# A decoder trunk in fp32 on one core: the end of its mixing layer by a table of units, two merge sums on VectorE, and eight columns in an existing slot

## The chip, the cores and the metric

The kernel runs on one core of one Trainium2 chip. The metric is device time in microseconds of one execution. Engines are named as in the profile: PE (TensorE matmul) and PEld (its weight loads), DVE (VectorE), ACT (ScalarE), POOL (GpSimd), SP (SyncE, which here issues most of the loads).

## The reference

One layer of a decoder trunk and a last norm, on x of 1 x 1024 x 1024 in float32:

```
h  = rmsnorm(x) @ w_in             # attention inputs and two gates of 1024 columns
ya = differential attention (4 heads x 2 x 64, causal, ALiBi)
yb = sliding-window attention (8 heads of 64, window 128, sinks)
m  = sigmoid(g0) * (ya @ w_br_da) + sigmoid(g1) * (yb @ w_br_sw)   # merge
x  = x + m @ w_mix_out             # mixing layer
u  = rmsnorm(x) @ w_up             # to 2 x 2816 columns
c  = causal depthwise conv of width 3 over u, plus bias
x  = x + (silu(gate) * val) @ w_down
out = rmsnorm(x)
```

## The kernel before

**Arithmetic.** Every float32 operand of a product is held as two fp32r tiles, high and low: a cast on ACT makes the high part and a subtraction on DVE the low part. A product takes three matmuls (high x high, high x low, low x high). The large products with weights are done by a scheme of seven products P1 to P7 in place of eight, on blocks A11, A12, A21, A22 of the weights and B11, B12, B21, B22 of the data: some factors are sums of blocks (S1 to S4 of the weights, T1 to T4 of the data), and the results are recombined. Data lie transposed: a partition is a channel, a tile of 128 channels by 1024 positions has two halves of 512.

**The merge** (`rest`, L839 to L875) makes m in eight steps of 128 channels. A step loads two gate tiles (`gr`), multiplies them by the norm's scale on POOL (L845), takes the sigmoid on ACT (L852), computes the two branch products on PE (L199 to L201, tiles `sc` and `g` in PSUM), gates them on DVE (L859, L861), and sums the two (L869, into `mr`): on POOL for steps 0 to 6, on DVE for step 7. Then it splits blocks of the sum into high (L882, ACT) and low (L883, DVE), and from step 4 on adds blocks in place by an accumulating DMA on POOL's queue (L889).

**The mixing layer** (`mix`, L891 to L1033) runs the seven products in the order P1, P2, P5, P6, P3, P7, P4, each in two halves: 14 halves, i = 0 to 13. A half loads and splits a weight (L178 cast on ACT, L180 low part on DVE), runs 24 matmuls (L1014) into two PSUM chains and adds them to the residual tile `xm[m]` on DVE (L1016). A chain of PSUM is used again by a later stage and so must be evicted first. A half of `xm[m]` becomes final in P2 (m = 0 to 3, first half), P3 (second half), P7 (m = 4 to 7, second half) and P4 (first half). `finish` then stores it (L935), squares it on ACT (L942) and adds the square to a sum on POOL (L943).

**The data of the up projection** are made from these finished halves, in code that `finish` puts off by one to three halves with `later`. For m < 4 the first half times the norm's weight gives B11 (L945), the second times the negative weight (`nw`, 8 columns; L947) is added to the first by an accumulating DMA (L930), and the sum is split into T1. For m > 3 the second half times the weight goes to a tile c (L951) and gives B22; it is added to both halves of `xm[m - 4]`, which gives T3 and T2. The first half times the negative weight (L956) gives B21, and added again T4. `put` splits a result: a cast on ACT (L919) and a low part on DVE (L920). T3 and B21 are put in tiles that the trace calls x0 to x7. `run_due(i)` runs what is due at half i, ahead of that half's matmuls; what is due at 14, 15 and 16 comes after the last.

**The first weights of the up projection** come from `part_pair` (L116): part 0 is A11 and A12, part 1 S1 and S2, part 2 S3 and S4, part 3 A22; each is a load on SP (L121), a cast on ACT (L126) and a low part on DVE (L128). Parts 1 and 2 are called in the two halves of P4 ahead of `run_due`, with a raised priority, parts 0 and 3 after P4.

**The up projection** (`hidden`, L1047) does for its first block of columns (j = 0) P1, P5, P3, P7, P2, then the sums of squares (L207), P6 and P4; a product is L1043. Then P1 and P2 of j = 1 follow, and the norm's scale is spread over the partitions by eight transposes (L222). The sums are recombined (L512 to L521) and go on to a scaling on POOL and the convolution.

**Order.** A scheduler reorders instructions of one engine by priority and by its own estimate of times; `tc.issue_after(x)` keeps an instruction behind x, `tc.high_priority` raises it. Semaphores for the data are added by the framework. Each engine works its list strictly in order. Pools give out buffers by tag and size, and an instruction that takes a buffer again waits for the last reader.

## Time and profile before

| | us |
|---|---|
| runs | 1348.41, 1350.07, 1350.72; median 1350.07 |
| the profiled execution | 1351.85 |
| its span in the trace | 1350.1, at a mean granted clock of 0.99 |
| the merge's last step and the mix's start | around 590 to 600 |
| the mix's end and the first products of the up projection | around 660 to 720 |

The span runs from the first to the last instruction; the execution's time holds 1.75 us more. Times in the text are microseconds from the span's start. A row of a timeline gives the start, the duration (of the whole group where it ends in x2 or more, first start to last end), engine, line, operation, output and inputs; in square brackets the time for which the engine idled before, and what ended that. A row of the waits gives who waited on whom: total, number, longest.

### The profile page before, as it was taken

What the parts mean: (1) busy time and instruction counts of PE and PEld (TensorE: products, weight loads), DVE (VectorE), ACT (ScalarE), POOL (GpSimd) and SP (SyncE); (2) the same over time, 40 slices, a digit from 0 to 9 for tenths busy, and PEclk for the clock granted to TensorE, in tenths of its full rate; (3) what the DMA queues carried; (4) which work ended last, traced back from release to release, by engine and by line L of the source; (5) the groups of instructions that cost most, each with busy time, mean ns of one, the idle gap of its engine ahead of it and who ended that gap; (6) DMA issues with size and microseconds to landing.
All of it is one profiled execution on the core that took longest, in us unless ns stands there. A gap on an engine that the chain in (4) does not pass through costs nothing.

```text
span 1350.1 us, 17338 instructions
## 1 busy us (share of the span) xinstructions
PE 1324.8 (98%) x6162; PEld 1088.5 (81%) x6162; DVE 1036.6 (77%) x1503; ACT 639.0 (47%) x1010; POOL 512.1 (38%) x412
## 2 busy tenths in 40 slices
PE   9999999999999999999969999999999999999997
PEld 7888888888888878878858888888888888888886
DVE  8836763389888975457579998989999988886855
ACT  9423232276667773335654343334333444554543
POOL 0447664001101016753355567766766622000002
PEclk9999999999999999999979999999999999999999
DMA  8356976966553245578694336554635227953434
GB/s 303 130 154 200 262 190 187 294 177 187 141 138 140 78 132 199 151 222 231 179 252 141 140 121 176 142 189 121 218 100 146 71 87 268 313 174 116 154 93 144
DMA packets 86598, 231.67 MB, mean 172 GB/s; under 512 B 9584, under 2 KB 17392, under 8 KB 86256
## 3 DMA queue, kind: packets, MB, share of 16 engines
q1 hardware_dynamic: 63264, 187.04, 41.4%
q0 software_dynamic: 10368, 26.22, 11.4%
q10 hardware_dynamic: 12880, 17.31, 3.7%
q8 instruction: 48, 0.79, 0.2%
q14 instruction: 38, 0.31, 0.1%
HBM read 173.39 MB, written 84.41 MB: 191 GB/s over the span
## 4 chain that ended last, share of the span: by engine, by line
PE 87%; POOL 4%; DMA 3%; DVE 2%; issue 2%; ACT 1%; SPq 0%; POOLq 0%; ACTq 0%; DVEq 0%
PE t L1043 44%; PE y L1263 9%; PE d L1263 7%; PE m L1014 4%; PE g L199 3%; PE g L200 3%; PE g L201 3%; PE sc L687 3%; POOL mr L869 2%; DMA gr<-gd 2%; POOL gr L845 2%; DMA xm<-xm 1%; PE t L703 1%; PE t L806 1%; PE sc L775 1%
## 5 line engine op out<-in xcount | busy, mean ns | idle before, releaser
L180 DVE TENSOR_TENSOR wl<-raw,wh 128x1024 fp32r<-128x1024 f32 (+2 forms) x91 | 100.0, 1100 | 70.9 <-ACT wh L178 58.2
L178 ACT CAST wh<-raw 128x1024 fp32r<-128x1024 f32 (+2 forms) x91 | 80.5, 884 | 111.8 <-PE y L1263 53.6
L157 ACT CAST sh<-sf 128x1024 fp32r<-128x1024 f32 x58 | 60.6, 1050 | 113.8 <-PE t L1043 99.5
L1193 POOL TENSOR_TENSOR us<-us,rstd 128x1024 f32<-128x1024 f32 x42 | 92.3, 2229 | 57.5 <-DVE us L520 31.8
L1043 PE MATMUL t<-T,sh 128*128 128x512 f32 x352 | 111.2, 397 | 0.0
L216 POOL TENSOR_TENSOR rs<-ms,mhalf 128x8 f32<-128x8 f32 (+2 forms) x9 | 13.7, 1519 | 240.6 <-DVE ms L214 234.5
L143 POOL TENSOR_TENSOR sf<-rv 128x512 f32<-128x512 f32 x29 | 53.3, 1837 | 110.2 <-DMA rv<-in_w_up 45.5
L1043 PE MATMUL t<-x,wh 128*128 128x512 f32 x248 | 84.8, 399 | 3.9 <-ACT x L919 3.9
L159 DVE TENSOR_TENSOR sl<-sf,sh 128x1024 fp32r<-128x1024 f32 x58 | 77.9, 1344 | 9.1 <-ACT sh L157 9.1
L1043 PEld LDWEIGHTS t<-T,sh 128*128 128x128 f32 x352 | 66.6, 190 | 15.4
L199 PE MATMUL g<-xh,wh 128*128 128x512 f32 x176 | 71.4, 405 | 1.5 <-ACT g L616 1.5
L200 PE MATMUL g<-x,wh 128*128 128x512 f32 x176 | 70.7, 402 | 0.0
L201 PE MATMUL g<-xh,wl 128*128 128x512 f32 x176 | 70.7, 401 | 0.0
L1210 DVE SCALAR_TENSOR_TENSOR c<-us,vecs,c 128x1024 f32<-128x1024 f32 x44 | 70.3, 1630 | 0.1
L1043 PE MATMUL t<-T,sl 128*128 128x512 f32 x176 | 69.3, 394 | 0.0
L1043 PE MATMUL t<-x,sh 128*128 128x512 f32 x212 | 68.4, 390 | 0.0
L1209 DVE SCALAR_TENSOR_TENSOR c<-us,vecs,c 128x1024 f32<-128x1024 f32 x44 | 66.0, 1537 | 1.2 <-ACT c L1207 1.2
L145 POOL TENSOR_TENSOR sf<-raw,rv 128x512 f32<-128x512 f32 x29 | 54.2, 1869 | 32.0 <-DVE sl L159 32.0
L1263 PE MATMUL y<-h,wh 128*128 128x512 f32 (+1 forms) x224 | 66.3, 379 | 0.0
L1014 PE MATMUL m<-x,wh 128*128 128x512 f32 x192 | 61.4, 401 | 1.8 <-DVE gr L861 1.8
L691 DVE CUSTOM_DVE_ANT_0 L<-sc,bias 128x128 f32<-128x128 f32 (+7 forms) x64 | 47.7, 752 | 17.0 <-PE sc L687 14.2
L670 POOL MEMSET aT<- 128x128 f32 x32 | 6.2, 205 | 142.9 <-PE t L716 102.0
(338 smaller groups left out, 4016.6 us busy)
## 6 DMA issues: line engine op xcount, KB each, us to landing
u<-qd SPq DMA_DIRECT2D x72, 256.0 KB, 6.1
raw<-in_w_in SPq DMA_DIRECT2D x22, 512.0 KB, 5.5
raw<-in_w_up SPq DMA_DIRECT2D x22, 512.0 KB, 4.7
hd<-c SPq DMA_DIRECT2D x22, 512.0 KB, 2.6
sdP<-in_w_down POOLq DMA_DIRECT2D x16, 704.0 KB, 8.3
rv<-in_w_up SPq DMA_DIRECT2D x20, 512.0 KB, 4.9
hc<-hd SPq DMA_DIRECT2D x33, 256.0 KB, 4.8
gr<-gd SPq DMA_DIRECT2D x16, 512.0 KB, 4.6
```

Of the source, the lines that this page charges most:

```text
L159: low = nc.vector.tensor_tensor(lo, src, hi.bitcast(F32), ALU.subtract)
L178: self.hi = nc.scalar.copy(wh, raw)
L180: self.lo = (eng or nc.vector).tensor_tensor(wl, raw, wh.bitcast(F32), ALU.subtract)
L199: nc.tensor.matmul(ps, wh[:, kc + o, :], ah, start=first and n == 0, stop=False)
L200: nc.tensor.matmul(ps, wh[:, kc + o, :], al, start=False, stop=False)
L201: nc.tensor.matmul(ps, wl[:, kc + o, :], ah, start=False, stop=last and n == len(kcs) - 1)
L1014: nc.tensor.matmul(ps, v[:, m % 2 * 4 + k, :], x, start=start and k == j == 0, stop=k == 3 and j == 2, skip_group_check=True)
L1043: nc.tensor.matmul(ps, (ah, ah, al)[p][:, k, :], (bh, bl, bh)[p], start=first and n == p == 0, stop=last and p == 2 and n == len(ks) - 1, ...
L1193: i = (nc.vector if m % NF == 0 else nc.gpsimd).tensor_tensor(us[:, 2:], us[:, 2:], self.rstd, ALU.mult)
L1209: nc.vector.scalar_tensor_tensor(c, us[:, 1:T + 1], cw[1], c, ALU.mult, ALU.add)
L1210: nc.vector.scalar_tensor_tensor(c, us[:, 0:T], cw[0], c, ALU.mult, ALU.add)
L1263: nc.tensor.matmul(ps, v[:, k - k0, :], x, start=start and k == i == 0, stop=k == HK - 1 and i == 2, skip_group_check=True)
```

## The change

**1. Merge sums.** L869 runs on DVE for steps 6 and 7 instead of step 7 alone.

**2. `nw`** is taken from the tag "ms" of its pool, whose tile of eight columns exists already (in `rstd_cols`), instead of a buffer of its own.

**3. The put-off work** is no longer collected in `finish`. Small functions for one unit each stand in a table `due`, by half: which function, for which k, in which order.

**4. B21** is made straight from the residual tile: the cast multiplies by `nw` (L921), and one DVE instruction multiplies and subtracts (L922). The scaled half for the addition is made apart (`scale3`), in the other half of the same tile.

**5. The first weights.** Part 0 (A11, A12) is called in half 13 ahead of `run_due`, parts 1 and 2 in the halves of P4 behind it, part 3 behind everything.

**6. Evictions** of halves 11 and 12 are kept behind the low part that `run_due` made last (`held`), those of the others behind the weight's low part (`first`), as is `finish` in half 13.

```diff
-                    (nc.vector if m == KC - 1 else nc.gpsimd).tensor_tensor(mr[:, m], gs[0], gs[1], ALU.add)
+                    (nc.vector if m > KC - 3 else nc.gpsimd).tensor_tensor(mr[:, m], gs[0], gs[1], ALU.add)
...
-        nw = self.st.tile([P, KC], F32, name="nw")
+        nw = self.tl(self.st, [P, KC], "ms")
...
-        later = lambda i, f: due.setdefault(i, []).append(f)
...
-            if m < 4 and hf == 0:
-                later(i + 2, lambda: (nc.scalar.mul(x, x, wcol(m)), put("B11", k, x)))
-            elif m < 4:
-                later(i + 2, lambda: (nc.scalar.mul(x, x, nw[:, m:m + 1]), add(col(k, 0), x)))
-                later(i + 3, lambda: put("T1", k, col(k, 0)))
-            elif hf:
-                t = x22[k // 2][:, k % 2]
-                later(i + 1, lambda: (nc.scalar.mul(t, x, wcol(m)), put("B22", k, t), add(col(k, 1), t)))
-                later(i + 2, lambda: (add(col(k, 0), t), put("T3", k, col(k, 1))))
-                later(i + 3, lambda: put("T2", k, col(k, 0)))
-            else:
-                t = col(m, 1)
-                later(i + 1, lambda: (nc.scalar.mul(t, x, nw[:, m:m + 1]), put("B21", k, t), add(col(k, 0), t)))
-                later(i + 2, lambda: put("T4", k, col(k, 0)))
+        def scale1(k):
+            x = col(k, 0)
+            nc.scalar.mul(x, x, wcol(k))
+            put("B11", k, x)
+
+        def scale2(k):
+            x = col(k, 1)
+            nc.scalar.mul(x, x, nw[:, k:k + 1])
+            add(col(k, 0), x)
+
+        c22 = lambda k: x22[k // 2][:, k % 2]
+
+        def scale4(k):
+            nc.scalar.mul(c22(k), col(k + 4, 1), wcol(k + 4))
+            put("B22", k, c22(k))
+
+        def sums4(k):
+            add(col(k, 1), c22(k))
+            add(col(k, 0), c22(k))
+
+        def scale3(k):
+            nc.scalar.mul(col(k + 4, 1), col(k + 4, 0), nw[:, k + 4:k + 5])
+            add(col(k, 0), col(k + 4, 1))
+
+        t1, t2, t3, t4 = (lambda k, n=n, h=h: put(n, k, col(k, h)) for n, h in (("T1", 0), ("T2", 0), ("T3", 1), ("T4", 0)))
+        b21 = lambda k: put("B21", k, col(k + 4, 0), nw[:, k + 4:k + 5])
+        due = {6: ((scale1, 0, 1),), 7: ((scale1, 2, 3),), 10: ((scale2, 0, 1),), 11: ((t1, 0, 1), (scale2, 2, 3), (scale4, 0, 1), (sums4, 0, 1)),
+               12: ((scale4, 2, 3), (t1, 2, 3), (sums4, 2, 3), (t3, 0, 1)), 13: ((t3, 2, 3), (t2, 0, 1), (b21, 0), (scale3, 0), (b21, 1), (scale3, 1)),
+               14: ((b21, 2), (t2, 2), (b21, 3), (t2, 3), (scale3, 2, 3), (t4, 0, 1), (t4, 2, 3))}
...
-                        if stage == "P4":
-                            self.uw = uw
-                            w0.update(self.part_pair(pair, 1 + h))
-                            self.uw = None
+                    if i == 13:
+                        w0.update(self.part_pair(pair, 0))
...
                     run_due(i)
+                    held = lows[-1] if lows else None
+                    first = self.lo
+                    if stage == "P4":
+                        self.uw = uw
+                        w0.update(self.part_pair(pair, 1 + h))
+                        self.uw = None
...
-                        tt(x, x, ps, ALU.subtract if o or stage == "P2" else ALU.add)
-                        if done:
-                            finish(i, m + o, hf)
+                        with tc.issue_after((held if 10 < i < 13 else first).ins):
+                            tt(x, x, ps, ALU.subtract if o or stage == "P2" else ALU.add)
+                        if last:
+                            with tc.issue_after(first.ins) if i == 13 else nullcontext():
+                                finish(m + o, hf)
...
-        with tc.high_priority(60):
-            for part in (0, 3):
-                w0.update(self.part_pair(pair, part))
         run_due(i)
-        run_due(i + 1)
-        run_due(i + 2)
+        w0.update(self.part_pair(pair, 3))
```

Lines behind L930 have other numbers after the change: L1014 is L1034, the eviction L1016 is L1037, L919 and L920 are L918 and L919, L942 and L943 are L941 and L942, L947, L951 and L956 are L951, L957 and L965, L1043 is L1061.

How it stands in the engines' lists, first on DVE at the merge's last two steps (a piece of the difference; gr tiles are the gates, x and m the split blocks, wl a weight's low part):

```order
 L859 SCALAR_TENSOR_TENSOR gr_5593<-gr_5593,g_5624 128x512
 L861 TENSOR_TENSOR gr_5593<-gr_5593,g_5638 128x512
+L869 TENSOR_TENSOR mr<-gr_5589,gr_5593 128x1024
 L180 TENSOR_TENSOR wl_5663<-raw_5659,wh_5661 128x1024
 L883 TENSOR_TENSOR x_1013_5653<-mr,x_1013_5653 128x512
 L883 TENSOR_TENSOR m_5136<-mr,m_5136 128x512
```

The sum of step 6 now stands on DVE behind its own last gate and ahead of a weight's low part; on POOL, where it stood behind the two L845 of step 7, it is gone.

Second, DVE where P7's last eviction meets P4's second weight (xm_5769 and xm_5770 are xm6 and xm7, T_0 and T_1 are T1 for k = 0 and 1, B_0 and B_1 are B22), before:

```order
L180 TENSOR_TENSOR wl_6270<-raw_6266,wh_6268 128x1024
L920 TENSOR_TENSOR T_0_5752<-xm_5763,T_0_5752 128x512
L1016 TENSOR_TENSOR xm_5769<-xm_5769,m_5788 128x512
L920 TENSOR_TENSOR T_1_5753<-xm_5764,T_1_5753 128x512
L1016 TENSOR_TENSOR xm_5770<-xm_5770,m_5789 128x512
L180 TENSOR_TENSOR wl_6330<-raw_6326,wh_6328 128x1024
L920 TENSOR_TENSOR B_0_5756<-c_5775,B_0_5756 128x512
L920 TENSOR_TENSOR B_1_5757<-c_5775,B_1_5757 128x512
```

And after:

```order
L180 TENSOR_TENSOR wl_6270<-raw_6266,wh_6268 128x1024
L919 TENSOR_TENSOR T_0_5752<-xm_5763,T_0_5752 128x512
L919 TENSOR_TENSOR T_1_5753<-xm_5764,T_1_5753 128x512
L180 TENSOR_TENSOR wl_6332<-raw_6328,wh_6330 128x1024
L919 TENSOR_TENSOR B_0_5756<-c_5775,B_0_5756 128x512
L919 TENSOR_TENSOR B_1_5757<-c_5775,B_1_5757 128x512
L1037 TENSOR_TENSOR xm_5769<-xm_5769,m_5788 128x512
L1037 TENSOR_TENSOR xm_5770<-xm_5770,m_5789 128x512
```

The two evictions moved behind the weight's low part and the two B22 splits.

Third, ACT from B22's first casts to the first cast of an S part (L126 sh), before (x_1093 and x_1094 are x0 and x1, from T3; c_5775 and c_5776 hold c0, c1 and c6, c7 in the text's words):

```order
L919 CAST B_1_5757<-c_5775 128x512
L935 DMA x2d<-xm_5769 128x512
L942 ACTIVATE sqs<-xm_5769 128x512
L935 DMA x2d<-xm_5770 128x512
L942 ACTIVATE sqs<-xm_5770 128x512
L935 DMA x2d<-xm_5767 128x512
L126 CAST sh_6334<-raw_6332 128x1024
L126 CAST sh_6392<-raw_6390 128x1024
L919 CAST T_2_5754<-xm_5765 128x512
L919 CAST T_3_5755<-xm_5766 128x512
L919 CAST x_1093_6343<-xm_5763 128x512
L919 CAST x_1094_6347<-xm_5764 128x512
```

And after:

```order
L918 CAST B_1_5757<-c_5775 128x512
L918 CAST T_2_5754<-xm_5765 128x512
L918 CAST T_3_5755<-xm_5766 128x512
L918 CAST x_1091_6348<-xm_5763 128x512
L918 CAST x_1092_6351<-xm_5764 128x512
L934 DMA x2d<-xm_5769 128x512
L941 ACTIVATE sqs<-xm_5769 128x512
L934 DMA x2d<-xm_5770 128x512
L941 ACTIVATE sqs<-xm_5770 128x512
L957 ACTIVATE c_5776<-xm_5769,vecs 128x512
L957 ACTIVATE c_5776<-xm_5770,vecs 128x512
L918 CAST B_2_5758<-c_5776 128x512
```

Both S casts left this place: S1 and S2's stands two rows further on, then a store and a square of each of xm4 and xm5, then A11 and A12's (wh), and S3 and S4's behind the T2 and B21 units of half 13. On POOL the four DMAs of c0 and c1 now follow the two of T1 directly, and the four of c6 and c7 each other.

The change to `nw` moves one DVE instruction of 128 x 8 from the program's start to the attention's end, and the scheduler puts the last sliding-window steps (the stretch from 410 to 490 us) in another order on DVE, PE and ACT: the same instructions, differently interleaved.

More of the change, by code (lines that the diff above doesn't have):

```diff
@@ L907, in mix @@
         x22 = [self.tl(self.cpl, [P, 2, H2], "c") for _ in range(2)]
-        nw = self.st.tile([P, KC], F32, name="nw")
+        nw = self.tl(self.st, [P, KC], "ms")
         nc.vector.tensor_scalar(nw, self.vecs[:, C_NF:C_NF + KC], -1.0, None, ALU.mult)
-        acc, nsq = self.rstd, []
+        acc, nsq, lows = self.rstd, [], []
         col = lambda m, hf: xm[m][:, hf * H2:(hf + 1) * H2]
         wcol = lambda m: self.vecs[:, C_NF + m:C_NF + m + 1]
-        due = {}
         def parts(t, src, scale=None):
@@ L919, in parts @@
                 nc.scalar.copy(hi, src)
-                tt(lo, src, hi.bitcast(F32), ALU.subtract)
+                low = tt(lo, src, hi.bitcast(F32), ALU.subtract)
             else:
                 nc.scalar.mul(hi, src, scale)
-                stt(lo, src, scale, hi.bitcast(F32), ALU.mult, ALU.subtract)
+                low = stt(lo, src, scale, hi.bitcast(F32), ALU.mult, ALU.subtract)
+            lows.append(low)
             return hi, lo
@@ L930, in mix, with finish @@
         add = lambda x, y: nc.gpsimd.dma_start(x, y, accum_op=ALU.add)
-        later = lambda i, f: due.setdefault(i, []).append(f)
-        def finish(i, m, hf):
+        def finish(m, hf):
             x, k = col(m, hf), m % 4
@@ L964, in run_due @@
             with tc.issue_after(self.hi.ins), tc.issue_after(self.lo.ins):
-                for f in due.pop(i, ()):
-                    f()
+                for f, *ks in due.pop(i, ()):
+                    for k in ks:
+                        f(k)
         plan = {"P1": ("B11", 1, True, 0, 0, False), "P2": ("B21", 0, True, 0, 0, True), "P5": ("T1", 0, True, 4, 1, False), "P6": ("T2", 1, False, 0, 1, False),
@@ L973, in mix @@
             for n, stage in enumerate(STAGES):
-                b, which, start, o, hf, done = plan[stage]
+                b, which, start, o, hf, last = plan[stage]
                 if stage == "P7":
```

## The prediction

> **What bounds the kernel now.** I read the page first, then PE's waits, then busy time by stage, then the timelines around the waits. The page's busy times, slices and waits of PE:
>
> ```profile
> PE 1324.8 (98%) x6162; PEld 1088.5 (81%) x6162; DVE 1036.6 (77%) x1503; ACT 639.0 (47%) x1010; POOL 512.1 (38%) x412
> PE   9999999999999999999969999999999999999997
> ...
> PE t L1043 <- ACT wh L126: 6.7, 1, 6.7
> PE t L1043 <- ACT x L919: 3.9, 1, 3.9
> PE m L1014 <- DVE gr L861: 1.8, 1, 1.8
> ```
>
> TensorE is busy 98% of the span, and one slice of 40 falls to 6. The three longest waits, 12.4 us together, are all in code that the diff touches: the last merge step (L861), and the mixing layer's end with the first products of the up projection (L126, L919). Busy time and granted clock of the stretches that hold them (length, then PE, PEld, DVE, ACT, POOL, the clock, DMA share and GB/s):
>
> ```profile
> 590.00:600.00 10.00, 8.20 (x34) 6.39 (x34) 6.41 (x9) 3.83 (x6) 5.14 (x3) 0.96 0.65 211
> 600.00:610.00 10.00, 10.00 (x39) 8.01 (x38) 5.67 (x8) 3.43 (x5) 0.88 (x1) 0.86 1.05 356
> ...
> 670.00:680.00 10.00, 5.80 (x25) 4.35 (x24) 9.12 (x9) 6.22 (x11) 5.76 (x6) 0.89 1.07 264
> 680.00:690.00 10.00, 7.53 (x22) 5.99 (x23) 10.00 (x13) 9.01 (x17) 7.21 (x8) 0.60 1.08 252
> 690.00:700.00 10.00, 7.79 (x34) 6.00 (x32) 6.17 (x6) 2.53 (x6) 3.56 (x3) 1.00 1.06 332
> 700.00:710.00 10.00, 8.32 (x30) 7.34 (x31) 5.58 (x7) 6.79 (x10) 5.72 (x4) 0.66 0.57 149
> ```
>
> A full-clock stretch grants 1.00, a half-clock one 0.5: so 0.96 and 0.86 make (0.04 + 0.14) × 10 × 2 = 3.6 us at half clock after the 1.8 us wait; 0.89 and 0.60 make 10.2 us, the last 8 of them up to about 688; 0.66 makes 6.8 us. PE's timeline at the ends of the stages:
>
> ```profile
> 593.92 0.62 PE L1014 MATMUL m<-x,wh 128*128 128x512 f32 x2
> ...
> 598.68 0.73 PE L1014 MATMUL m<-x,wh 128*128 128x512 f32 x2 [1.80 <-DVE gr L861]
> ...
> 675.41 0.40 PE L1014 MATMUL m<-x,wl 128*128 128x512 f32 x1
> 682.47 1.22 PE L1043 MATMUL t<-B,wh 128*128 128x512 f32 x2 [6.66 <-ACT wh L126]
> ...
> 701.68 0.80 PE L1043 MATMUL t<-x,wh 128*128 128x512 f32 x1 [3.89 <-ACT x L919]
> ...
> 718.58 0.63 PE L1043 MATMUL t<-x,wh 128*128 128x512 f32 x2
> ...
> 719.27 1.03 PE L222 MATMUL t<-ident,rs 128*128 128x128 f32 x8
> ```
>
> The last rows give a warm matmul's price: two at 718.58 and one behind them fill the time to 719.27, 0.23 us each. The mix's 336 (14 halves of 24) from 593.92 would end at 671.8; they end at 675.6: 3.9 lost, 1.8 by the wait and half of 3.6 by the clock. From 675.6 to L222 at 719.27 lie 43.6 us: 108 matmuls L1043 (25.0) and some 2 us of L207, so 16.6 are lost: 6.66 + 3.89 waiting, and about (688 − 682.5)/2 + 6.8/2 = 6.2 by the clock. **At most about 21 us are to be had.** After 719.27 I read PE as full, so what is won there stays won.
>
> **The merge end.** The step for m = 6 and the last gate, on POOL, ACT and DVE:
>
> ```profile
> 586.16 4.76 POOL L845 TENSOR_TENSOR gr<-gr,rstd 128x1024 f32<-128x1024 f32 x2 [2.95 <-DMA gr<-gd]
> 590.89 3.37 POOL L869 TENSOR_TENSOR mr<-gr,gr 128x1024 f32<-128x1024 f32 x1
> ...
> 590.95 1.06 ACT L852 ACTIVATE gr<-gr 128x1024 f32<-128x1024 f32 x1 [0.37 <-POOL gr L845]
> ...
> 585.62 0.68 DVE L861 TENSOR_TENSOR gr<-gr,g 128x512 f32<-128x512 f32 x1
> ...
> 594.94 0.69 DVE L883 TENSOR_TENSOR x<-mr,x 128x512 fp32r<-128x512 f32 x1 [2.94 <-ACT x L882]
> ...
> 597.95 0.68 DVE L861 TENSOR_TENSOR gr<-gr,g 128x512 f32<-128x512 f32 x1
> 598.66 1.23 DVE L869 TENSOR_TENSOR mr<-gr,gr 128x1024 f32<-128x1024 f32 x1
> ```
>
> Now the sum's operands are ready at 586.3 (585.62 + 0.68), but it stands on POOL behind two L845 until 590.89 and takes 3.37; its casts follow at 594.3, and DVE's last gate (597.95 to 598.6), which frees the PSUM tile for which PE waits, stands behind the splits L883. On DVE it costs 1.23 and could end at 587.5. The casts then follow the sigmoid of 590.95 on ACT: casts 592.0 to 593.1, splits 592.6 to 593.9, four gates of 0.6, the last done at 596.35. PE wants it at 596.7: no wait. The price that no row shows is this DVE sum beside POOL's L845. Below: 1.23 and POOL unhurt. Above: it blocks and is blocked, as in this pair with its undisturbed like:
>
> ```profile
> 675.45 4.13 DVE L920 TENSOR_TENSOR T<-xm,T 128x512 fp32r<-128x512 f32 x2
> ...
> 681.30 1.28 DVE L920 TENSOR_TENSOR B<-c,B 128x512 fp32r<-128x512 f32 x2
> ...
> 675.76 3.27 POOL L943 TENSOR_TENSOR rstd<-rstd,sqs 128x512 f32<-128x512 f32 x2
> ```
>
> Two DVE splits took 4.13 beside POOL's adds, 1.28 without. So above, the sum ends at 589.8, POOL's second L845 and the sigmoid come a microsecond later, and the last gate ends at 597.35: a wait of 0.65, so short that I expect no half-clock stretch. I win 3.9 less 0.65: **3.2**, between 3.2 and 3.9. The Trainium skill, "SBUF — State Buffer", section "SBUF: two separate sides", states that a DVE operation with two SBUF inputs and a GpSimd operation that reads SBUF share an exclusive port lock for the whole instruction. The 4.13 agrees; by that rule the upper price holds. The skill's "TensorE: Matmul & The Clock Gate", Part 1, would have half clock only after an idle window of about 3.4 us; here 1.80 sufficed, so the row decides.
>
> **The mix's stages.** Their weights, products and evictions keep their places, so they move up with the 3.2, except P7's eviction of xm6 and xm7:
>
> ```profile
> 665.87 0.68 DVE L1016 TENSOR_TENSOR xm<-xm,m 128x512 f32<-128x512 f32 x1
> ...
> 668.67 1.23 DVE L180 TENSOR_TENSOR wl<-raw,wh 128x1024 fp32r<-128x1024 f32 x1 [2.12 <-ACT wh L178]
> ```
>
> It stood ahead of the last weight split (L180); now it stands behind that split and two B22 splits, which wait for ACT's scales, which wait for the second accumulating DMA. By the durations above it ends at about 668.5, where PE (3.2 earlier) wants its PSUM tile at 666.8: **a new wait of 1.75**, with a half-clock stretch some 3.5 in all. I count it at nothing: the up projection cannot start before about 681 anyway, as follows, so the mix may end at 672.4 or 675.9. If that cover were gone it would cost the 3.5.
>
> **The chain to the up projection.** ACT, then POOL's accumulating DMAs and their time from issue to landing (min, median, max):
>
> ```profile
> 664.61 0.62 ACT L919 CAST T<-xm 128x512 fp32r<-128x512 f32 x1 [1.70 <-DMA xm<-xm]
> 665.13 1.33 ACT L947 ACTIVATE xm<-xm,nw 128x512 f32<-128x512 f32 x2
> 666.37 1.32 ACT L951 ACTIVATE c<-xm,vecs 128x512 f32<-128x512 f32 x2
> ...
> 672.09 2.00 ACT L126 CAST sh<-raw 128x1024 fp32r<-128x1024 f32 x2 [1.37 <-DVE xm L1016]
> ...
> 678.07 0.62 ACT L919 CAST x<-xm 128x512 fp32r<-128x512 f32 x1 [2.41 <-DMA xm<-c]
> ...
> 681.39 1.55 ACT L126 CAST wh<-raw 128x1024 fp32r<-128x1024 f32 x2
> ...
> 666.26 1.78 POOL L930 DMA_DIRECT2D xm<-xm  x2 [1.93 <-DVE T L920]
> ...
> DMA to landing us min/median/max: 3.4/6.8/9.7
> ```
>
> Before, ACT cast the S parts (672.09), then waited for x1's sum (T3) to land (678.07), did c6, c7 and B22, and only then cast A11 at 681.39, on which PE's 6.66 ends. After, c0 and c1 lead to six accumulating DMAs in a row on POOL (two T1, four T3 and T2). The second T1 lands at 664.61 − 3.2 = 661.4; one cast, two scales and two c (0.6 + 1.3 + 1.3) later the issues begin at about 663.1, 0.67 apart: x1's T3 is the fifth, issued at 665.7. Its landing I take as 8.1 us, between the median 6.8 and the maximum 9.7 since six are under way: 673.8. Behind it ACT has x1's cast, two squares, c6, c7, two B22, the S1/S2 cast (half of 2.00) and two squares: 10 × 0.6 + 1.0, so A11 is cast from 680.6 to 681.6, against 681.39 to 682.42. The early load of A11 thus gains ACT only 0.8.
>
> The larger change is behind it. PE starts P1 at 681.7. The S3/S4 cast, before done at 674.1, now stands behind six T3, T2 and B21 casts and four scales, and ends near 690.4, its low part 691.9. So P1 and P5 (12 matmuls each, at half clock to 688, then full) end at 690.5 and P3 waits 1.4, ending 694.3; P7 697.0, P2 699.8. **The 3.89 us wait and its 3.4 us of half clock go**, as x6 and x7 are made by one ACT and one DVE instruction straight from xm (L921, L922), ahead of scale3. Then L207 to 701.5, P6 704.3, P4 707.1. Late next is j = 1's first weight (A11, cast behind both S pairs): ready at about 709.8, a wait of 2.7; its products end at 712.6 and, with P2 of j = 1, L222 starts between 714.9 and 716.6, I take 715.2. Against 719.27 that is **−4.1**. The merge's 3.2 is in this sum already (as the start 661.4), not to be added.
>
> **The rest.** The tile nw in a slot of "ms" moves one small DVE instruction (128x8, too short to matter) from the program's start to the attention's end, and with it the scheduler's order of the last sliding-window steps. PE and DVE there:
>
> ```profile
> 410.00:490.00 80.00, 77.91 (x445) 64.75 (x445) 74.41 (x244) 58.78 (x162) 7.36 (x27) 1.00 0.33 106
> ```
>
> PE idles 2.1 of 80 us, so at most 2.1 can be won; DVE is at 93%, so a worse order could lose about as much. I take 0, ±2. B21 by one scaled split instead of scale and split saves nothing that is waited for elsewhere.
>
> **The sum.** 1351.85 (the profiled execution: the span 1350.1 and 1.75 around it) − 4.1 = 1347.75. The profiled execution lies 1.8 over the median of the runs, 1350.07, so against that I predict **1346.0**. A change within 0.2%, 2.7 us, is about what a measurement of this kernel cannot tell from none.
>
> **Rivals.** *Slower: the six DMAs in a row block ACT.* Five transfers precede x1's cast, which stands ahead of all weight casts of the up projection on ACT. Software transfers by queue, 655 to 705:
>
> ```profile
> q0 software_dynamic: 2258, 4.14, 48.3%
> ```
>
> 4.14 MB took 48.3% of 50 us, so five of 16 transfers take 7.6 us if they have the engines to themselves, and landing follows; at half of the engines 15.2 after 663.1, at 678.3, 4.5 later than I assume, which leaves +0.4. Slower by over 2.7 from a landing at 680.6 on; at a share of 0.4 it is 682.1 and +4.2: **1354.2**. For it: the DMA share of 1.06 to 1.08 in these stretches. Against it: the longest of all landings so far was 9.7. Chance 0.18.
>
> *No change: gains are given back.* The merge is won, but P7's eviction and the late S3/S4 cast make new waits, and L222 comes 1 to 2 us earlier or as before: **1349**. For it: the 16.6 us lost are a chain of casts and DMAs on ACT and POOL that the merge doesn't shorten, and DVE is full (10.00 of 10) from 680 to 690. Against it: the wait for x6 and x7 is cut by construction. Chance 0.22.
>
> *A bigger gain.* x1 lands in 5 us instead of 8.1, P1 starts 3 us sooner and j = 1's weight with it; half clock ends earlier: −8.5, **1341.5**. Chance 0.15; the forecast's own case has 0.45 (1343.5 to 1347.3).
>
> **How the numbers follow.** Faster by over 0.2%: 0.45 + 0.15 = 0.60; within: 0.22; slower: 0.18. The range leaves out half of the slower case and the end of the bigger gain: 1340 to 1353.5, which takes in the attention's ±2 and the landing's 6.8 to 9.7.
>
> **What would show it.** Right: in the profile after, no wait of PE on L861 and full clock from 590 to 610; the mix ending between 672 and 676 with a wait of 1 to 2 us for xm6's eviction; a first product of the up projection at 681 ± 2 with a wait for the A11 cast of 6 to 9 us; no wait on x6 or x7; a short wait in P3 and one of 2 to 3 us at j = 1's first weight. Wrong: landings of L930 over 12 us; or a first product before 677, which would mean that the early A11 load decides after all; or a PE idle time over 4 us between 410 and 490.

## The result, and the profile after

The changed kernel takes **1337.77 us** in the median of four runs (1336.39 to 1340.05), the kernel before beside it 1349.58 (1348.41 to 1350.72): a ratio of 0.9914, interval 0.9897 to 0.9931, so 11.8 us faster. That is nearly three times the forecast of 4.1 and 2.2 us below the end of its range. The profiled execution took 1337.29 us, with a span of 1335.5.

The page and PE's longest waits after:

```profile
PE 1307.9 (98%) x6162; PEld 1086.4 (81%) x6162; DVE 1059.9 (79%) x1504; ACT 637.6 (48%) x1010; POOL 513.5 (38%) x411
PE   9999999999999999999979999999999999999997
...
PE t L1061 <- ACT wh L126: 7.0, 2, 5.5
PE m L1034 <- DVE xm L1037: 2.4, 1, 2.4
PE g L199 <- DVE u L518: 1.8, 1, 1.8
PE t L361 <- DVE x L359: 1.5, 1, 1.5
PE t L1061 <- ACT sh L126: 1.4, 1, 1.4
PE g L199 <- ACT g L616: 1.4, 4, 0.5
PE t L1061 <- DVE wl L128: 1.4, 1, 1.4
```

The waits on L861 and on x are gone, and new ones stand in their place: the eviction L1037, the S parts, a weight's low part. PE's *busy* time is 16.9 us less (1324.8 to 1307.9) for the same 6162 records of matmuls. Another order of the units can remove idle time, and stretches at half clock here and there, but those are no fewer at the mix's end: 17.0 us of them from 660 to 720 before, 17.1 after. The stretches after, with the columns of before:

```profile
590.00:600.00 10.00, 10.00 (x46) 8.28 (x45) 8.10 (x11) 3.25 (x4) 0.88 (x1) 1.00 0.94 327
600.00:610.00 10.00, 10.00 (x46) 8.29 (x45) 6.29 (x10) 3.49 (x6) 2.67 (x3) 1.00 1.04 350
660.00:670.00 10.00, 7.64 (x27) 5.87 (x26) 5.43 (x8) 5.24 (x9) 5.27 (x6) 0.83 0.90 177
670.00:680.00 10.00, 4.43 (x16) 2.84 (x16) 6.17 (x8) 7.48 (x12) 5.86 (x7) 0.82 0.76 187
680.00:690.00 10.00, 7.73 (x26) 5.65 (x27) 8.08 (x10) 7.08 (x12) 5.65 (x6) 0.84 0.99 247
690.00:700.00 10.00, 10.00 (x44) 8.22 (x42) 7.14 (x8) 5.13 (x9) 3.99 (x4) 0.83 0.98 263
700.00:710.00 10.00, 7.47 (x35) 5.38 (x34) 4.16 (x6) 3.72 (x5) 0.99 (x3) 1.00 0.54 172
710.00:720.00 10.00, 9.69 (x39) 7.89 (x40) 7.99 (x11) 4.08 (x6) 8.04 (x7) 0.83 0.40 138
```

The merge's end is full and at full clock now. The mix's end still holds 13 us of idle PE (660 to 720), and its half-clock stretches have only moved. PE's timeline after, around it:

```profile
665.65 0.78 PE L1034 MATMUL m<-x,wh 128*128 128x512 f32 x2 [2.36 <-DVE xm L1037]
...
678.49 1.22 PE L1061 MATMUL t<-B,wh 128*128 128x512 f32 x2 [5.53 <-ACT wh L126]
688.04 0.73 PE L1061 MATMUL t<-B,sh 128*128 128x512 f32 x2 [1.43 <-ACT sh L126]
...
717.07 1.03 PE L222 MATMUL t<-ident,rs 128*128 128x128 f32 x8
```

L222 starts at 717.07 against 719.27: of the 14.6 us by which the spans differ, 2.2 have been won here. The rest arises behind it, in the up and the down projection, where PE's list is the same before and after. A piece of the mix in the timelines of before and after:

```profile
629.63 0.62 PE L1014 MATMUL m<-x,wh 128*128 128x512 f32 x2
...
631.72 0.39 PE L1014 MATMUL m<-x,wh 128*128 128x512 f32 x1
```

```profile
629.81 0.62 PE L1034 MATMUL m<-x,wh 128*128 128x512 f32 x2
...
631.17 0.62 PE L1034 MATMUL m<-x,wh 128*128 128x512 f32 x2
```

Before, nine matmuls take 2.09 us (629.63 to 631.72), 0.232 each; after, six take 1.36 (629.81 to 631.17), 0.227 each, both at a granted clock of 1.00. And in before's own merge, six take 1.36 as well:

```profile
590.29 0.39 PE L201 MATMUL g<-yh,wl 128*128 128x512 f32 x1
...
591.65 0.39 PE L201 MATMUL g<-yh,wl 128*128 128x512 f32 x1
```

So the pitch, the time from one matmul's start to the next one's, differs by 2.5% for the same form of matmul between stages of one execution. What differs is where the operands lie. In the compiled programs the weight tiles wh start at bytes 21632 and 25728 of a partition before, and at 21504 and 25600 after, 128 lower; so do all tiles of the left side of SBUF behind the small pool that held `nw` (four buffers of 32 bytes). The tiles x0 to x7 lie on the right side and haven't moved, at multiples of 512. Sorting all matmuls by the addresses of the moving operand and of the next weights gives, for before (the merge with its counts):

```
stage                      moving mod 256   next weights mod 256   mean pitch
project (0 to 250 us)            0                 128               232.3 ns
merge (500 to 584), 341        128                 128               226.7
                     29          0                 128               232.4
mix (600 to 660)                 0                 128               232.4
up projection (720 to 1100)    0 or 128         the same             227.6
                               0 or 128         the other            233.0
```

After, in the merge, the mix and the up projection, both are at 0 and the pitch is 226.7 ns; in the project stage it is 226.7 to 227 as well. The theory to test was: **the gain comes from the addresses, which `nw`'s move shifted, and the new order of the units is worth nothing or less.** The rival: the gain comes from the order and the merge sum, as forecast.

### The profile page after: what moved, and what is told of

It reads as the page before. It is cut to its first block, busy times and chain, and to the rows that moved or that the text cites. A ratio compares the mean times of both kernels' runs of the same rounds, so it can differ in the third digit from the quotient of the medians.

```text
span 1335.5 us, 17341 instructions
## 1 busy us (share of the span) xinstructions
PE 1307.9 (98%) x6162; PEld 1086.4 (81%) x6162; DVE 1059.9 (79%) x1504; ACT 637.6 (48%) x1010; POOL 513.5 (38%) x411
## 4 chain that ended last, share of the span: by engine, by line
PE 83%; POOL 4%; DMA 4%; issue 3%; DVE 2%; ACT 2%; SPq 0%; POOLq 0%; ACTq 0%; DVEq 0%
PE t L1061 34%; PE y L1281 9%; PE d L1281 7%; PE g L199 4%; PE g L200 4%; PE g L201 4%; PE m L1034 4%; PE sc L687 3%; POOL us L502 2%; PE t L703 1%; PE sc L201 1%; PE sc L200 1%; PE sc L199 1%; PE t L806 1%; PE sc L775 1%
## 5 line engine op out<-in xcount | busy, mean ns | idle before, releaser
L180 DVE TENSOR_TENSOR wl<-raw,wh 128x1024 fp32r<-128x1024 f32 (+2 forms) x91 | 107.8, 1186 | 48.9 <-ACT wh L178 40.9
L1211 POOL TENSOR_TENSOR us<-us,rstd 128x1024 f32<-128x1024 f32 x42 | 95.4, 2319 | 48.3 <-DVE us L520 29.1
L1061 PE MATMUL t<-T,sh 128*128 128x512 f32 x352 | 108.5, 390 | 0.0
L143 POOL TENSOR_TENSOR sf<-rv 128x512 f32<-128x512 f32 x29 | 60.0, 2070 | 105.9 <-DMA rv<-in_w_up 48.0
L1225 ACT ACTIVATE c<-us,vecs 128x1024 f32<-128x1024 f32 x44 | 54.7, 1247 | 78.3 <-POOL us L1211 73.9
L159 DVE TENSOR_TENSOR sl<-sf,sh 128x1024 fp32r<-128x1024 f32 x58 | 74.2, 1280 | 10.7 <-ACT sh L157 10.7
L1061 PE MATMUL t<-x,wh 128*128 128x512 f32 x248 | 82.2, 389 | 0.0
L1061 PEld LDWEIGHTS t<-T,sh 128*128 128x128 f32 x352 | 65.9, 188 | 13.6
L1228 DVE SCALAR_TENSOR_TENSOR c<-us,vecs,c 128x1024 f32<-128x1024 f32 x44 | 71.2, 1651 | 0.1
L1227 DVE SCALAR_TENSOR_TENSOR c<-us,vecs,c 128x1024 f32<-128x1024 f32 x44 | 68.5, 1585 | 2.6 <-ACT c L1225 2.6
L1061 PE MATMUL t<-T,sl 128*128 128x512 f32 x176 | 68.5, 389 | 0.0
L1061 PE MATMUL t<-x,sh 128*128 128x512 f32 x212 | 68.2, 389 | 0.0
L159 DVE TENSOR_TENSOR wl<-raw,wh 128x1024 fp32r<-128x1024 f32 x29 | 63.8, 2199 | 0.1
L1034 PE MATMUL m<-x,wh 128*128 128x512 f32 x192 | 60.3, 396 | 2.4 <-DVE xm L1037 2.4
```

The source lines that it names most:

```text
L159: low = nc.vector.tensor_tensor(lo, src, hi.bitcast(F32), ALU.subtract)
L180: self.lo = (eng or nc.vector).tensor_tensor(wl, raw, wh.bitcast(F32), ALU.subtract)
L1034: nc.tensor.matmul(ps, v[:, m % 2 * 4 + k, :], x, start=start and k == j == 0, stop=k == 3 and j == 2, skip_group_check=True)
L1061: nc.tensor.matmul(ps, (ah, ah, al)[p][:, k, :], (bh, bl, bh)[p], start=first and n == p == 0, stop=last and p == 2 and n == len(ks) - 1, ...
L1211: i = (nc.vector if m % NF == 0 else nc.gpsimd).tensor_tensor(us[:, 2:], us[:, 2:], self.rstd, ALU.mult)
L1227: nc.vector.scalar_tensor_tensor(c, us[:, 1:T + 1], cw[1], c, ALU.mult, ALU.add)
```

## Experiments: addresses against order

The kernels have an unused tile at either end of SBUF, of LPAD and RPAD bytes. Changing LPAD moves all left tiles and changes no instruction and no order. (It also moves the small constant tiles ahead of the pool of `nw`, which the change leaves in place.)

**e1**, before at the addresses of after:

```diff
-LPAD, RPAD = 480, 480
+LPAD, RPAD = 352, 480
```

> The kernel before, with the padding tile at the left end of SBUF 128 bytes smaller (LPAD 352 instead of 480): every engine has the same instructions in the same order as before, and all tiles of the left side, the weight tiles wh and wl among them, lie at the addresses that they have in the changed kernel. Theory (addresses): the changed kernel's gain comes from the matmul's pitch, which the traces show as 0.2324 us where the addresses of the moving operand and of the next weights differ by 128 bytes modulo 512, and as 0.2267 us where they agree. Then this kernel alone gains as much as the change or a little more: 1335 to 1339 us, with a pitch of 0.2267 us in the mix and in the up projection. Rival (schedule): the gain comes from the merge sum and the table of units; then this kernel takes the time of before, 1349.6 +-1.5.

Measured: 1336.1 us (five runs, 1334.04 to 1341.01) against 1351.0 for before, measured beside it; ratio 0.9903, interval 0.9885 to 0.9921. The addresses alone do what the whole change does.

**e2**, after at the addresses of before:

```diff
-LPAD, RPAD = 480, 480
+LPAD, RPAD = 608, 480
```

> The changed kernel with the left padding 128 bytes larger (LPAD 608): the same instructions in the same order as after, at the addresses of before. Theory (addresses): the gain is gone; what is left is the schedule alone, which by the shift between the traces of before and after (5.6 us ahead at the mix's start, 2.2 ahead when the up projection runs, of which about 4 come from the pitch) is worth nothing or a loss of 2: 1349 to 1352 us, the pitch again 0.2324 us in the mix. Rival (schedule): it stays at 1337.8 +-1.5.

Measured: 1354.6 us (twelve runs, 1351.31 to 1357.87) against 1351.0; ratio 1.0026, interval 1.0015 to 1.0037. At unchanged addresses the change is 3.6 us **slower**, beyond the loss of up to 2 that the address theory allowed. A window of 200 us in the up projection, of before, e1 and e2 in turn (length, PE busy and its matmuls, then the other engines):

```profile
800.00:1000.00 200.00, 200.00 (x870) 162.87 (x868) 181.78 (x165) 79.26 (x83) 132.96 (x95) 1.00 0.52 155
```

```profile
800.00:1000.00 200.00, 200.00 (x884) 165.59 (x883) 193.77 (x168) 80.63 (x85) 134.64 (x97) 1.00 0.52 154
```

```profile
800.00:1000.00 200.00, 200.00 (x869) 162.77 (x868) 192.08 (x166) 81.81 (x83) 136.38 (x94) 1.00 0.52 154
```

PE is busy all the time in all three; e1 fits in 884 matmuls, before and e2 870 and 869 (after: 884). The start of the same matmul of the program in the four traces, in us (the last is the 6000th of 6102):

```
                          before      e1     after      e2
project, the 800th        189.21   186.03   187.31   189.65
merge, the 2800th         566.49   562.68   564.98   569.61
mix, the 3200th           662.39   655.31   655.65   662.91
L222 (the norm's scale)   719.27   712.99   717.07   722.94
down, the 6000th         1324.83  1306.91  1311.03  1328.47
L222 to the 6000th        605.56   593.92   593.96   605.53
```

The last row: 11.6 us less in the two kernels at the lower addresses, whichever the order of the units, and nothing between the two orders at either address. Up to the merge the same order of instructions differs by up to 3.5 us from execution to execution (the 2800th matmul at 562.68 in e1, at 566.20 in e9), in small waits of PE for casts and loads, so single rows there aren't to be read that closely.

**m1**, the pitch by itself:

```diff
+for name, wo, vo in runs:          # weights wo, moving operand vo bytes past a multiple of 512
+    for n in range(48):
+        a, b = wo // 4 + n % 2 * 128, vo // 4
+        nc.tensor.matmul(t, w[:, a:a + 128], v[:, b:b + H2], start=n == 0, stop=n == 47)
```

> Not the decoder: it leaves the whole computation out and copies x to the output. It runs groups of 48 matmuls of 128x128 by 128x512 in fp32r, as the decoder's, with nothing else at work; weights at a multiple of 512 bytes, the moving operand 0, 32, 64, 96, 128, 160, 192, 224, 256, 320, 384, 448 and 512 bytes past one; then both 128 past, both 64 past, and the weights alone 128 and 64 past; a group each, warm. Theory (TensorE's own two reads disturb each other by their relative address): 0.2267 us each at 0 and 512 and where both are moved alike, 0.232 at 128 and 384 and with the weights alone 128 past; the others are open and give the period. Rival (the address matters only beside the reads and writes of other engines): 0.2267 us in all groups.

Measured, with no other engine at work but a copy per group. The rows are windows from the start of a group of 48 to the start of the next: the moving operand 0, 32, 64, 128, 256, 384 past, both 128 past, and the weights alone 128 past (the counts include a matmul that reaches in from the group before):

```profile
20.44:31.32 10.88, 10.88 (x49) 9.01 (x48) 0.69 (x1) 0.00 (x0) 0.00 (x0) 1.00 0.01 2
31.32:42.52 11.20, 11.20 (x49) 9.00 (x48) 0.69 (x1) 0.00 (x0) 0.00 (x0) 1.00 0.00 0
42.52:53.52 11.00, 11.00 (x49) 9.01 (x48) 0.69 (x1) 0.00 (x0) 0.00 (x0) 1.00 0.00 0
64.73:75.93 11.20, 11.20 (x49) 9.01 (x48) 0.69 (x1) 0.00 (x0) 0.00 (x0) 1.00 0.00 0
109.56:120.44 10.88, 10.88 (x49) 9.01 (x48) 0.69 (x1) 0.00 (x0) 0.00 (x0) 1.00 0.01 2
131.44:142.60 11.16, 11.16 (x49) 9.04 (x48) 0.69 (x1) 0.00 (x0) 0.00 (x0) 1.00 0.00 0
...
164.71:175.59 10.88, 10.88 (x49) 9.01 (x48) 0.69 (x1) 0.00 (x0) 0.00 (x0) 1.00 0.01 2
186.48:197.62 11.14, 11.14 (x49) 9.04 (x48) 0.69 (x1) 0.00 (x0) 0.00 (x0) 1.00 0.00 0
```

10.88 / 48 = 0.2267 us where the two addresses agree modulo 256, wherever both lie; 11.00 to 11.20 (0.229 to 0.2333) where they don't. Both 64 past: 0.227; the groups of 96, 160, 192, 224 and 448 past have 0.233 to 0.234, 320 past 0.229, 512 past 0.227, and the weights alone 64 past 0.233. So the addresses of TensorE's own two operands are enough; no other engine is needed, and the rival falls. Why equal addresses are the good case isn't shown.

**e8**, the period in the real kernel: e3 (below) with LPAD 96, which lowers all left tiles by another 256 bytes.

> e3 with the left padding another 256 bytes smaller (LPAD 96): the same instructions in the same order; the left tiles lie 256 past a multiple of 512, those of the right side at 0. Theory with a period of 512: the pitch is 0.232 us again in the mix, and the time 15 to 18 us above e3, 1348 to 1352 us. Theory with a period of 256: as e3, 1333 us.

Measured: 1335.69 us (1332.7 to 1336.68), ratio 0.9879, interval 0.9863 to 0.9894, with a pitch of 226.7 ns in the mix. The period is 256; nothing of the 15 to 18 us comes back.

## Experiments: what the order and the merge sum are worth

**e3**, e1 with the merge sum of step 6 on VectorE, and **e4**, after without it:

```diff
-                    (nc.vector if m == KC - 1 else nc.gpsimd).tensor_tensor(mr[:, m], gs[0], gs[1], ALU.add)
+                    (nc.vector if m > KC - 3 else nc.gpsimd).tensor_tensor(mr[:, m], gs[0], gs[1], ALU.add)
```

> e1 with one more edit: the merge sum of step 6 on VectorE, everything else as in e1. Theory: the 1.8 us wait of PE on L861 and its half-clock stretch (3.9 us lost together at the start of the mix) go; whether that reaches the end is open, since the up projection's start waits for a chain of casts and accumulating DMAs that starts with the mix's results and so moves up with it: 3 to 4 us less than e1. Rival (the chain at the mix's end does not move up because its DMAs or the casts hold it): within 1 us of e1.

> The changed kernel with the merge sum of step 6 back on GpSimd. Theory: the 1.8 us wait on L861 and the half-clock stretch come back, and with them 3 to 4 us: 1341 to 1342 us. Rival (the table of units hides it, as the up projection waits for its first weights anyway): within 1 us of the changed kernel, 1337.8.

Measured: e3 1333.25 us (1332.01 to 1334.35), ratio 0.9869, interval 0.9854 to 0.9884; 2.85 below e1, measured beside it, with intervals that barely don't overlap. e4 1340.04 us (1337.37 to 1342.97), ratio 0.992, interval 0.9905 to 0.9936, 2.3 above after, which overlaps with after's. From the 2880th matmul to the 2960th, the merge's end, e3 takes 1.7 us less than e1, and after 1.5 less than e4. The sum is worth 1.5 to 3 us, less than either expectation: PE's wait on L861 is 1.65 us in e1 and 1.20 in e4, and the half-clock stretch that both had counted follows neither. And e3, which has the old order of units, takes 4.5 us less than the changed kernel, with an interval clear of its own: it beats both, and what the change holds besides the addresses and the merge sum costs time.

**e5**, after with one wait taken out, the eviction of half 11:

```diff
-                        with tc.issue_after((held if 10 < i < 13 else first).ins):
+                        with tc.issue_after((held if i == 12 else first).ins):
```

> The changed kernel with the evictions of half 11 behind the weight's low part (as those of the other halves) and not behind the last low part of the put-off work. Theory: PE's 2.4 us wait for the eviction of xm6 and its half-clock stretch go, and c6, c7 and their B22 move ahead of x0 and x1 on ScalarE, so that the cast of A11 stands 2.4 us nearer to x1's landing: 1 to 2.5 us less than the changed kernel. Rival (as predicted: the wait is covered by the wait for A11): within 1 us of it.

Measured: 1335.4 us (1334.97 to 1337.96), ratio 0.9884, interval 0.9869 to 0.9899: 2.4 below after, as the theory said, though the intervals touch. In the profile the mix's wait is gone, and the first L1061 starts at 679.37 in place of 678.49 in an execution that ran 3.4 us behind at the 3200th matmul, so 2.6 sooner by its own measure; L222 follows at 714.23, by that measure 6.3 sooner. This moves the eviction and also c6 and c7 on ACT; which of the two it is stays open.

**e7**, e5 with all casts of the first weights ahead of x0 and x1:

```diff
-               12: ((scale4, 2, 3), (t1, 2, 3), (sums4, 2, 3), (t3, 0, 1)), 13: ((t3, 2, 3),
+               12: ((scale4, 2, 3), (t1, 2, 3), (sums4, 2, 3)), 13: ((t3, 0, 1, 2, 3),
...
                     if i == 13:
                         w0.update(self.part_pair(pair, 0))
+                        self.uw = uw
+                        w0.update(self.part_pair(pair, 2))
+                        self.uw = None
...
-                    if stage == "P4":
+                    if i == 12:
                         self.uw = uw
-                        w0.update(self.part_pair(pair, 1 + h))
+                        w0.update(self.part_pair(pair, 1))
```

> e5, and the splits x0 and x1 (T3, k = 0 and 1) put off from half 12 to half 13, S3 and S4 called with A11 ahead of half 13's put-off work: on ScalarE all three casts of the first weights stand ahead of x0 and x1, whose sums land late. Theory (PE's wait for A11 comes from the wait for x1's landing, which stands ahead of A11 on ScalarE): the first product of the up projection starts when the mix ends, at 671 to 674 us instead of 678.5, and P3 no longer waits for its S parts; 4 to 8 us less than the changed kernel. Rival (the landings of T3, T2 and T4 set the end, whatever the casts' place): the wait moves from A11 to x0 to x7 or T4, and the time stays within 1.5 us of e5.

Measured: 1338.96 us (1336.02 to 1342.73), ratio 0.991, interval 0.9892 to 0.9928: nothing gained, though the first half of the theory holds. PE's waits in e7:

```profile
672.04 0.73 PE L1064 MATMUL t<-B,wh 128*128 128x512 f32 x2 [0.73 <-ACT wh L126]
676.38 0.80 PE L1064 MATMUL t<-B,wl 128*128 128x512 f32 x1 [3.60 <-DVE wl L128]
689.48 0.70 PE L1064 MATMUL t<-x,sh 128*128 128x512 f32 x2 [2.71 <-DVE xm L1040]
...
704.85 0.51 PE L1064 MATMUL t<-T,wh 128*128 128x512 f32 x1 [3.37 <-ACT T L918]
```

The up projection starts at 672.04, 6.4 us sooner, and then waits for its weight's low part on DVE, for an eviction, and for T4, whose cast on ACT idles 7.82 us for a landing. The rival is right in kind, the wait for A11 is covered by what comes behind it; by size it isn't, as the median lies 3.6 us above e5's, though the intervals overlap.

**e9**, e3 with the work after the mix in another order, and **e10**, e9 with the changed kernel's B21:

```diff
-                for f in due.pop(i, ()):
+                fs = due.pop(i, ())
+                for f in fs[:2] + fs[4:] + fs[2:4] if i == 14 else fs:
                     f()
...
-                later(i + 1, lambda: (nc.scalar.mul(t, x, nw[:, m:m + 1]), put("B21", k, t), add(col(k, 0), t)))
+                later(i + 1, lambda: (put("B21", k, x, nw[:, m:m + 1]), nc.scalar.mul(t, x, nw[:, m:m + 1]), add(col(k, 0), t)))
```

(The first piece is e9's, both are e10's.)

> e3, with what is due after the mix in another order: T2 for k = 2 and 3, then B21 for k = 2 and 3 (x6 and x7), then T4 for k = 0 and 1; in e3 T4 stands ahead of B21, and its two casts wait on ScalarE for landings of accumulating DMAs (2.62 and 1.57 us, rows at 691.01 and 693.20) with x6 and x7 behind them. Theory (this order makes PE's 4.2 us wait on L919): the wait goes and with it some half clock, 3 to 6 us less than e3: 1327 to 1330 us. Rival (the next thing is late: T4 for P4 or the weights of the second block of columns): within 1.5 us of e3, 1333.

> e9, and B21 by the changed kernel's direct way (a cast that multiplies, and one scaled subtraction on VectorE) ahead of the scale for the sum. Theory: x6 and x7 come one ScalarE scale (0.6 us) sooner, and the sums for T4 later by one; the time is within 1 us of e9. Rival (the direct way is what the changed kernel gains by): 2 us or more less than e9.

Measured: e9 **1329.47 us** (1328.59 to 1331.65) against 1349.35 for before, ratio 0.9844, interval 0.981 to 0.9878; e10 1329.94 (1328.92 to 1332.74), ratio 0.9856, interval 0.9819 to 0.9892, the same within the interval; both came as expected, so the direct B21 adds nothing that shows. PE's first matmul on x6, which is in P2, and L222 in e3; then the first product, L207 and L222 in e9, where P2 runs through to L207 without a wait:

```profile
695.61 0.80 PE L1043 MATMUL t<-x,wh 128*128 128x512 f32 x1 [4.21 <-ACT x L919]
...
712.91 1.03 PE L222 MATMUL t<-ident,rs 128*128 128x128 f32 x8
```

```profile
677.38 1.22 PE L1044 MATMUL t<-B,wh 128*128 128x512 f32 x2 [6.83 <-ACT wh L126]
...
695.10 1.84 PE L207 MATMUL t<-ones,rstd 128*128 128x1 f32 x16
...
709.62 1.03 PE L222 MATMUL t<-ident,rs 128*128 128x128 f32 x8
```

The 4.21 us wait for x6 is gone, and L222 comes 3.3 us sooner in an execution that was 1.9 behind at the merge; the medians differ by 3.8, though the intervals of e3 and e9, which were not measured side by side, overlap. (With x6 and x7 early, the scheduler also puts PE's products on them ahead of L207; in e3 most of them stand behind it.) So what the table was to bring is had by one change of order, since x6 and x7 needn't stand behind T4's landings. e9 is the fastest kernel of this study, 8.3 us below the changed one.

The orders can be told apart more closely than by medians in the traces, by the time from the 3200th matmul to L222, in us:

```
before's order of units          before 56.88   e1 57.68   e3 57.71   e8 57.32
after's                          after  61.42   e4 61.19   e2 60.03
after's, evictions early         e5     55.15
e5's, weights' casts first       e7     60.76
before's, x6 and x7 ahead of T4  e9     52.76   e10 53.10
```

Kernels with the same order and the same addresses modulo 256 agree here within 0.4 us. As it stands, the table costs 3.7 us against e3's order; with half 11's evictions early it wins 2.6, and e9's order wins 5.0. So it is not the table as such that costs, but where it keeps those evictions and, with them, c6 and c7. Besides, the attention's new order costs 1.0 to 1.7 us (below), which e5 pays too and e3 doesn't.

## Why the prediction was wrong

**The step that failed** is the one on `nw`: "moves one small DVE instruction (128x8, too short to matter) from the program's start to the attention's end", taken as 0 ±2. Its effect was not an instruction but a place: four buffers of 32 bytes less in a small pool moved every tile behind it by 128 bytes. That was worth 14.9 us with the old order (e1) and 16.8 with the new (after against e2; 15.1 when each is set against the before measured beside it). `nw` in its new slot was not run by itself; e1 and e2 separate its addresses from all order. Nothing in the order of instructions could show it, and the order was what I had read. The trace of before could have: I took the warm matmul's price as 0.23 from three rows, and PE's rows hold 0.2267 in the merge and 0.232 in the mix, at the same clock. A price that is not constant at constant clock was the thing to explain. The bounds "at most about 21 us are to be had" and "what is won there stays won" counted idle PE only and took PE's busy time, 98% of the span, as given.

**The sum for the rest had the wrong sign.** e2 tests it by itself: forecast −4.1, measured +3.6 (interval +2.0 to +5.0 of 1351). In the traces e2 loses 3.1 us on before up to the 2880th matmul (1.0 of it in the attention, the rest within what executions differ by), wins 2.6 in the merge's end, and loses 3.15 from the 3200th to L222, where the forecast had won 0.9. Step by step, in e2, whose pitch is the one I reckoned with:

- *The merge sum.* The price of the DVE sum beside POOL's L845 lay between my bounds or at the upper one: 3.42 us in e2, 2.08 in after, with POOL's pair at 5.74 instead of 4.76. After's rows, DVE and POOL:

```profile
582.45 2.08 DVE L869 TENSOR_TENSOR mr<-gr,gr 128x1024 f32<-128x1024 f32 x1
...
581.06 5.74 POOL L845 TENSOR_TENSOR gr<-gr,rstd 128x1024 f32<-128x1024 f32 x2 [3.02 <-DMA gr<-gd]
```

  The wait was 0.76 in e2 (0.65 forecast as the upper case), without half clock. I booked 3.2; between the 2880th and the 2960th matmul e2 won 2.6 on before, and 1.5 to 1.7 was had at the lower addresses. Right in kind, too large.
- *P7's eviction.* A wait of 1.75 was forecast; 2.36 was measured in after, 1.08 in e2. "I count it at nothing" was too cheap by e5, which is 2.4 us faster without it in the median and 6.3 from the 3200th matmul to L222, though other instructions moved too.
- *The chain to A11.* The second T1's cast came at 664.59 in e2 (forecast 661.4, plus the 3.1 behind), the DMAs were not 0.67 apart but 0.7 to 2.4, x1 landed 6.4 us after its issue instead of 8.1, and from its landing to A11's cast it took 5.8 us instead of 6.8 (the sum writes ten casts of 0.6 where the list names nine). These errors cancel, by luck: A11 was cast at 683.63 to 684.7 (forecast 680.6 to 681.6, plus 3.1). The four DMAs of c0 and c1 followed the two of T1 directly in before too; what is new is that T2's first stands ahead of T3's second, which makes x1's the fifth.
- *The waits behind it.* The wait for x6 and x7 went, as forecast. P3 waited 1.83 and 0.84 (forecast 1.4 in one).
- *The end.* Here the sum broke: L222 was to start 33.5 us after the first L1061 (681.7 to 715.2); in e2 it came 38.2 after (684.71 to 722.94). PE and ACT in e2:

```profile
694.43 0.73 PE L1061 MATMUL t<-B,sh 128*128 128x512 f32 x2 [1.83 <-ACT sh L126]
696.00 0.79 PE L1061 MATMUL t<-B,sl 128*128 128x512 f32 x1 [0.84 <-DVE sl L128]
...
714.19 0.74 PE L1061 MATMUL t<-B,wh 128*128 128x512 f32 x2 [0.92 <-ACT wh L126]
716.31 0.79 PE L1061 MATMUL t<-B,wl 128*128 128x512 f32 x1 [1.39 <-DVE wl L128]
```

```profile
689.32 0.62 ACT L918 CAST x<-xm 128x512 fp32r<-128x512 f32 x1 [3.29 <-DMA xm<-c]
...
693.35 1.03 ACT L126 CAST sh<-raw 128x1024 fp32r<-128x1024 f32 x1
...
701.10 1.05 ACT L126 CAST sh<-raw 128x1024 fp32r<-128x1024 f32 x1 [0.62 <-DMA raw<-ud]
706.58 0.62 ACT L918 CAST T<-xm 128x512 fp32r<-128x512 f32 x1 [4.43 <-DMA xm<-xm]
711.14 0.62 ACT L918 CAST T<-xm 128x512 fp32r<-128x512 f32 x1 [3.95 <-DMA xm<-xm]
```

  Of the 4.7 us, 2.5 were lost by the end of P3, 0.6 at T4, 1.4 at j = 1's first weight (0.2 behind it). P3's waits came to 2.7, and a half-clock stretch of 3.4 us followed them, where the sum had full clock from 688 on. The S3/S4 cast stands behind x3, for whose landing ACT idled 3.29 us, where I had counted casts and scales alone. At j = 1's first weight PE waited 2.3, less than the 2.7 forecast, though it came there 3.2 later; again 3.4 us at half clock followed. T4 for k = 2 and 3 stood ahead of that weight on ACT and idled 8.4 us for two landings, where I had it wait for a load only. They are those of the last two scale3, which the table puts behind the T2 units of half 14 and whose DMAs POOL issues between additions, at 698.72 and 701.25. So the two terms that the sum put at nothing are half clock after these waits, and the rival's mechanism, a landing that blocks ACT in order, at places further on than x1.
- *The attention's new order* cost 1.0 to 1.7 us: from the 2000th to the 2400th matmul the five kernels with after's order take 70.8 to 71.5, the six with before's 69.7 to 69.9. It was in the ±2.

That the time came out on the forecast's side, faster, was luck: the work of a term that I had at zero. Six of the nine signs set down for "right" came true in after (missed: xm6's wait, 2.36; the first product, 678.49; the wait for A11, 5.53) and none of those for "wrong"; they all watched waits, granted clock and order, and none PE's price.

## What to carry to other kernels

An edit that frees or adds a buffer, however small, moves tiles; compare the tiles' addresses of the two programs before reading the order of instructions, and try a padding tile as an experiment of its own. Where an engine is busy 98% of the span, ask first whether its price per instruction is the same in all stages at the same clock, and sort it by operand when it isn't. Where an in-order engine casts results of DMAs, what stands behind the last landing is late next: put the work that waits for nothing ahead of it.

## What the runs showed of the hardware

- A matmul of 128x128 by 128x512 in fp32r, warm, takes 0.2267 to 0.2272 us when the moving operand and the weights start at equal addresses modulo 256 bytes of a partition, and 0.229 to 0.234 when they don't (m1, nothing else at work). Whether it is a matmul's own weights or the next ones that count isn't told apart: they nearly always agree modulo 256, and the 39 matmuls of before's up projection where they don't take 229.2 ns, between the two. All offsets tried that weren't a multiple of 256 cost 1 to 3%; on this kernel that was some 15 us.
- In the attention (300 to 490 us) the pitch is about 0.231 us in after too, where both operands lie at multiples of 256. Smaller matmuls and transposes stand between them there; why it is so was not tried.
- In each of the eleven traces of the decoder the granted clock changes only at steps of a grid of 3.413 us. Sort the windows between these steps, without the first 20 us and the last 15, by how long PE idled in them: a half-clock stretch follows each of the 25 windows at full clock with 1.80 us or more, and none with 1.61 or less; of the two between, 1.69 us (e4) had one behind it and 1.78 us (after, at 236) none. So the length of one wait doesn't tell. The 2.36 us in after gave a stretch of 3.4 us (0.83 in the row 660 to 670), as did the 1.80 of before, and 1.43 and 0.84 together in after; e7's wait of 2.71 us, which lies across a step, gave none, nor did e1's 1.65 on L861.
